# Low parts of 44 weight tiles made by ScalarE and an adding DMA instead of VectorE, with changed numbers and a changed choice in the instruction scheduler

## The chip, the cores and the metric

One core of one Trainium2 chip runs the whole program. The metric is the device time of one execution in microseconds. Five engines take part: PE (TensorE, matmuls), DVE (VectorE), ACT (ScalarE), POOL (GpSimd) and SP (SyncE, which begins the loads). Each engine works through its own list of instructions in order and waits at the head of the list for what other engines must deliver.

## What is computed

The reference is a chain of two blocks on 512 tokens of width 1024, in float32. The part that matters here is layer A of the second block:

```
u, qm, gate = split_cols(x @ a_w_in, (2 * 1536, 512, 2048))
a, gl = split(u, 2)                       # 1536 channels each
h = a * sigmoid(gl)
h = depthwise_conv(h, 31 taps, causal) + conv_b
y_mix = silu(layer_norm(h, g, b))         # over the 1536 channels
y_mem = memory cross attention of qm      # 4 heads
y = concat(y_mix, y_mem) * silu(gate)
x = layer_norm(ALPHA * x + y @ a_w_out)
```

Ahead of it stand a state-space mixer, a cross attention and a gated feed-forward layer; behind it stands layer B (an attention over selected keys).

## The kernel before

Activations lie with channels on the 128 partitions and the 512 tokens along the free dimension. A dense layer is done in tiles of 128 output channels: one tile of weights is 128 x 1024 numbers (512 KB), and `dense` runs 24 matmuls on it (8 slices of the input, 3 matmuls each: high part by high part, high by low, low by high), since float32 values are carried as two parts of a shorter type. `prep` makes the two parts: SP loads `raw`, ACT copies it to the high part `whi`, and DVE subtracts, `wlo = raw - whi`. There are 3 buffers for `raw` and 4 each for `whi` and `wlo`. PSUM has three banks `mm` for dense tiles, two each of `A` and `B`, one `C`.

Layer A takes 44 such tiles with the names `a_gl`, `a_a` (12 each), `a_qm` (4) and `a_gate` (16). `conv_tile` treats 128 channels: two dense tiles, then the 31 taps, of which ACT makes 11 products that POOL adds up (10 additions of 128 x 512), PE does one with a diagonal matrix into a bank `B`, and DVE does 19 in that bank. `LN` then centres the tiles and adds up their squares on POOL. When all 12 tiles are through, `lnc.finish` makes the statistics (matmuls into `C`), two rows are spread over the partitions, DVE and ACT normalise the 12 tiles, POOL multiplies by the gates, and the output layer `a_wo` follows.

The order of the instructions isn't that of the code. Every call is recorded as an `Op` with an estimated duration; `order` places them by a list schedule, engine by engine, with due times that are improved in `FBI` = 12 rounds by a schedule of the reversed program (`latest`); `emit` keeps the best round and issues the instructions in its order. All of them bear the line of `emit` in the profile (L378), so the rows are told apart by the names of their tiles. A number behind a name, as in `wlo1640`, is the number under which the tile was recorded; `raw1638`, `whi1639` and `wlo1640` are the three buffers of one tile of weights. Memory for a tile is taken when its first instruction is issued, and an instruction that finds no free buffer or bank waits.

Of the kernel before, what the change touches and what calls it, by code (L numbers as in the profile page):

```python
# [27 lines left out]
BIG = 1e30  # L28
WAHEAD = 400
WINDOW = 1500  # L30
SSD = 600
# [16 lines left out]

# [1 line left out]
ENGINES = ("PE", "ACT", "DVE", "POOL", "SP")  # L50
SWITCH, FBI, LATE, REUSE, MIX = 40000, 12, 850, 160, 0.5
LATENCY = {("PE", "PE"): 0.0, ("ACT", "ACT"): 0.0, ("DVE", "DVE"): 130.0, ("POOL", "POOL"): 102.0,
# [6 lines left out]
class View:  # L59
    """a lazily resolved access pattern of a tile"""  # L60

# [55 lines left out]
class Op:  # L117
    __slots__ = ("eng", "fn", "args", "kw", "outs", "ins", "deps", "succ", "prio", "dur", "port", "table", "new", "need", "idx",
                 "start", "end", "tiles", "m")


class Program:
    """records instructions in program order, then orders each engine's by a list schedule"""

# [12 lines left out]
    def rec(s, eng, fn, m, args, kw):  # L137
# [27 lines left out]
        if eng == "PE":  # L165
            one = m == "transpose" or args[1].base.dt == F32R
            o.table = n > 8
            o.dur = n / 2.4 * 2 if m == "transpose" else max(107, n / 2.4) + 2.5 if one else max(27, n / 2.4) * 4
        elif eng == "ACT":
            ptr = sum(isinstance(kw.get(k), View) for k in ("scale", "bias", "accum_out"))  # L170
            o.dur = n * 0.833 + 93 + 93 * ptr - 40 * (isinstance(args[1], View) and args[1].base.psum)
            o.table = _TABLE.get(args[2])
        elif eng == "DVE":
            two = m in ("tensor_tensor", "scalar_tensor_tensor")
            psum = any(x.psum for x in o.tiles)
            wide = [x for x in ins if int(np.prod(x.shape[1:])) > 1]
            ptr = len(ins) - len(wide)
            if m == "reciprocal":
                o.dur = n * 8.3 + 60
            elif m in ("tensor_reduce", "max", "match_replace"):  # L180
                o.dur = int(np.prod(wide[-1].shape[1:])) * 1.042 + 68
            elif not two and not psum:
                o.dur, o.port = n * 0.521 + 68 + 61 * ptr, n > 8
            else:
                o.dur = n * 1.042 + 68 + 61 * min(ptr, 1)
                o.port = two and sum(not x.base.psum for x in wide) == 2 and n > 8
        elif eng == "POOL":
            o.dur, o.port = (958 if kw.get("op") == ALU.pow else n * (2.2 if len(ins) > 1 else 1.0) + 99), n > 8
        else:
            o.dur = n * int(out.shape[0]) * 4 / 360.0  # L190
# [5 lines left out]
    def latest(s, prio):  # L196
        """latest starts, from a list schedule of the reversed program"""
        ops = s.ops
# [7 lines left out]
        while events:  # L206
# [4 lines left out]
            for e, q in ready.items():  # L211
                if busy[e] > now or not q:
                    continue
                o = ops[q[0][1]]
                if o.port and port > now:
                    heapq.heappush(events, port)
                    continue
                heapq.heappop(q)
                end = now + (o.dur + 1500 if e == "SP" else o.dur)
                busy[e] = now + o.dur  # L220
                if o.port:
                    port = end
                heapq.heappush(events, busy[e])
                when[o.idx] = -end
                for d in o.deps:
                    when[d] = max(when[d], end + s.latency(ops[d], o))
                    need[d] -= 1
                    if need[d] == 0:
                        heapq.heappush(wait, (when[d], -prio[d], d))
                        heapq.heappush(events, when[d])  # L230
        return when

    def order(s, prio, window):
# [4 lines left out]
        for o in ops:  # L238
            for x in o.tiles:
                left[x] = left.get(x, 0) + 1  # L240
                first.setdefault(x, o.idx)
                last[x] = o.idx
        # slots in use if the rest ran in program order: a tile may take one early only if this never exceeds the number there is
        live = {g: np.zeros(len(ops) + 1, np.int32) for g in free}
# [17 lines left out]
        while len(seq) < len(ops):  # L262
# [29 lines left out]
            for e, q in ready.items():  # L292
# [47 lines left out]
                if e == "SP":  # L340
                    hw = max(now, hw) + 450
                    dma = max(hw + 650, dma) + dur
                    o.end = dma + LATE
                    busy[e] = now + 60
                else:
                    o.end = now + dur
# [10 lines left out]
        return seq, max(o.end for o in ops), [o.start for o in ops]  # L357

    def emit(s, window):
        def real(a):  # L360
# [5 lines left out]
        prio = [o.prio * 200.0 for o in s.ops]  # L366
        best = r = s.order(prio, window)
        for it in range(FBI):
# [3 lines left out]
            r = s.order(w, window)  # L372
            if r[1] < best[1]:
                best, prio = r, w
        for o in best[0]:
# [5 lines left out]
def body(ctx, tc, t, out):  # L381
# [37 lines left out]

# [1 line left out]
    mhalf = const("mhalf", (P, 1))  # L421
# [21 lines left out]

# [1 line left out]
    def prep(src, kt, w=P):  # L445
        raw = new(wp, (P, 8 * P), F32, "raw")
# [5 lines left out]
        S.activation(hi[:, :n], raw[:, :n], AF.Copy)  # L452
        V.tensor_tensor(lo[:, :n], raw[:, :n], f(hi[:, :n]), op=ALU.subtract)
        prog.shift -= WAHEAD
# [13 lines left out]
    def wrange(name, mt, kt, k0=0):  # L468
        r = []
        while kt > 0:  # L470
            n = min(kt, 8)
            r += prep(t[name][mt][:, k0 * P:(k0 + n) * P], n)
            k0 += n
            kt -= n
        return r
# [17 lines left out]

# [1 line left out]
    def tok_sum(tiles, n=T):  # L495
# [27 lines left out]
    class LN:  # L523
        """layer norm over tiles that come one by one, centred first by the mean of the first npil tiles, whose sum is then 0"""

# [28 lines left out]
        def finish(s):  # L554
            """broadcast rows r, q with norm = centred * r - q"""
            ps = bank("C")
# [34 lines left out]
    NOFF, NPE = 11, 1  # L591
    # ================= block 1, mixer =================
    def load_x():
# [25 lines left out]

    # time steps of all heads  # L620
    raw = act()[:, :P]
# [28 lines left out]
    V.tensor_tensor(v3(dtr), v3(dtr), dtb.rearrange("p (o k) -> p o k", o=1).to_broadcast([P, 4, 16]), op=ALU.add)  # L650
    # softplus(x) = max(x, 0) + log1p(exp(-|x|)), log1p(e) = 2 atanh(e / (2 + e))
    ex, den, s2, po = s64(), s64(), s64(), s64()
# [18 lines left out]
    acs, cdec, dec = den, s2, s64()  # L671
    # cumulated steps as rows of heads
    ps = bank("B")[0:16, :]
# [14 lines left out]

    # causal convolution of xs, B, C; order of the channel tiles: B0 B1 C0 C1, then xs
    conv = {}  # L690
# [13 lines left out]

    # z gate
    zs = []
# [5 lines left out]

    # B in token rows, B C products
    triu_b = triu.rearrange("p (o k) -> p o k", o=1).to_broadcast([P, 4, P])
# [83 lines left out]

    # multi-scale pool
    icnt = const("icnt", (P, 64))  # L800
# [56 lines left out]

    # keys and values of the first memory
    def load_mem(src):
# [74 lines left out]

    # normalised SSD branch
    yhl = [split_g(conv[j], vc("ssd_norm", j)) for j in range(8)]
# [10 lines left out]

    # ================= block 1, cross attention =================
    def cols(x, b):
        return [a[:, b * P:(b + 1) * P] for a in x]  # L950

    class XAttn:
        """two heads (2 pr, 2 pr + 1) of 4; q: nd tiles [dims, T] per head; scale(tb): a number or a column per token"""

# [56 lines left out]
    def weave(*lists):  # L1011
        """emits the lists of steps in turns, each spread evenly over the longest"""
        n = max(len(x) for x in lists)
# [39 lines left out]

    # ================= block 1, swiglu =================
    rB = tok_bcast(rsq(tok_sum([ss.acc]), D, EPS))
# [23 lines left out]

    # taps of layer A: sigmoid(x) = (1 + tanh(x / 2)) / 2, and the half goes to the taps; some as diagonal matrices  # L1080
    cwh = vec2[:, 0:372]
# [38 lines left out]

    # ================= final norm of block 1 =================
    rB = tok_bcast(rsq(tok_sum([ss.acc]), D, EPS))
# [6 lines left out]
    MS = 128.0 ** -0.5  # L1129
    # ================= block 2, layer A =================  # L1130
    K0 = NOFF + NPE if NPE else NOFF + 1
# [39 lines left out]
    def gate_tile(w, j, half=False):  # L1171
        """silu(gate); with half, twice that from tanh"""
        ps = dense(wrange(w, j, 8), u)
# [13 lines left out]
    def out_tile(w, j, part, first, ln=None):  # L1187
        """part: the operands by row tile"""
        ks = sorted(part)
# [35 lines left out]

    # ================= block 2, layer B =================
    NQ0 = 6
# [101 lines left out]

    # token rows for the last layer norm  # L1330
    yN = [[act(), act()] for _ in range(4)]
# [48 lines left out]

    # last projection, token rows
    grow, brow = [act(), act()], [act(), act()]
# [151 lines left out]
```

## Time and profile before

| | before |
|---|---|
| timed runs | 1705.31, 1707.87, 1709.99 us (median 1707.87) |
| profiled execution, first to last instruction | 1705.8 us |
| median of the timed runs less that span | 2.1 us |
| PE busy | 1665.2 us (98%) |
| DVE busy | 1142.2 us (67%) |
| ACT busy | 775.9 us (45%) |
| POOL busy | 421.0 us (25%) |
| DMA engines busy, queue of the loads | 28.2% |

No time is given for the profiled execution beside its span, so sums are made in the span, and the 2.1 us to the median are added at the end. Busy shares are means over stages with different limits; an engine that is 67% busy overall can be full for a long stretch. PE's busy time is that of overlapping, pipelined matmuls, so a busy PE may still run at half its clock.

### The profile page before, as it was taken

The numbers are of one execution on the slowest core, as the hardware profiler recorded it, in microseconds if no ns is written. First come the engines' busy times: TensorE is split into PE (matmuls) and PEld (weight loads), VectorE is DVE, ScalarE is ACT, GpSimd is POOL, SyncE is SP. The second block draws the span as 40 slices with busy tenths as digits, with TensorE's granted clock in tenths as the row PEclk, the third lists the DMA queues.
The fourth block names the chain that finished last, engine by engine and source line by source line (L and its number), as shares of the span: only waits on it lengthen the run. The fifth ranks groups of instructions, "written<-read, shape, count | busy, mean of one in ns | idle before, by whom it ended". The sixth has DMA issues, their size and how long they took to land. (4 is left out here: it accounts for less than half of the span.)

```text
span 1705.8 us, 21241 instructions
## 1 busy us (share of the span) xinstructions
PE 1665.2 (98%) x7966; PEld 1361.4 (80%) x7966; DVE 1142.2 (67%) x1801; ACT 775.9 (45%) x1349; POOL 421.0 (25%) x325
## 2 busy tenths in 40 slices
PE   9999999999999999999999997999899999999998
PEld 7888678888888888888878775778787788788886
DVE  7836778574565435544477999988747895467754
ACT  6722444444553222332356766545435434545541
POOL 1004433020031001201233678965630000000000
PEclk9999999999999999999999998999999999999999
DMA  7321212531242333322323311232233123211121
GB/s 242 117 86 56 93 50 87 160 99 50 75 131 93 98 99 99 95 79 90 117 91 108 102 56 50 81 127 87 75 124 115 62 99 94 80 63 50 53 84 50
DMA packets 49719, 156.32 MB, mean 92 GB/s; under 512 B 5648, under 2 KB 7568, under 8 KB 49616
## 3 DMA queue, kind: packets, MB, share of 16 engines
q1 hardware_dynamic: 49616, 154.96, 28.2%
q8 instruction: 63, 1.03, 0.3%
q14 instruction: 40, 0.33, 0.1%
HBM read 152.71 MB, written 2.10 MB: 91 GB/s over the span
## 5 line engine op out<-in xcount | busy, mean ns | idle before, releaser
L378 PE MATMUL mm<-act,whi 128*128 128x512 f32 (+1 forms) x3888 | 1194.3, 388 | 18.5 <-DVE act L378 12.9
L378 PEld LDWEIGHTS mm<-act,whi 128*128 128x128 f32 x3888 | 717.8, 189 | 174.3 <-ACT act L378 15.3
L378 PE MATMUL mm<-act,wlo 128*128 128x512 f32 (+1 forms) x1944 | 749.4, 388 | 9.8 <-DVE wlo L378 9.6
L378 ACT ACTIVATE whi<-raw 128x1024 fp32r<-128x1024 f32 (+3 forms) x293 | 289.4, 991 | 582.0 <-PE mm L378 352.5
L378 POOL TENSOR_TENSOR act<-act,act 128x512 f32<-128x512 f32 (+1 forms) x252 | 372.5, 1493 | 683.7 <-DVE act L378 314.8
L378 DVE TENSOR_TENSOR wlo<-raw,whi 128x1024 fp32r<-128x1024 f32 (+3 forms) x293 | 373.2, 1281 | 123.7 <-ACT whi L378 118.9
L378 PEld LDWEIGHTS mm<-act,wlo 128*128 128x128 f32 x1944 | 366.9, 189 | 85.5 <-DVE wlo L378 11.3
L378 DVE TENSOR_TENSOR act<-mm,act 128x512 f32<-128x512 f32 (+3 forms) x173 | 114.6, 664 | 244.9 <-PE mm L378 236.9
L378 ACT ACTIVATE act<-act 128x512 f32<-128x512 f32 (+2 forms) x222 | 134.7, 617 | 104.6 <-DVE act L378 65.9
L378 DVE SCALAR_TENSOR_TENSOR B<-pad,vec,B 128x512 f32<-128x512 f32 x228 | 167.2, 753 | 5.7 <-PE B L378 1.5
L378 DVE TENSOR_TENSOR act<-act,act 128x512 f32<-128x512 f32 (+3 forms) x203 | 138.3, 711 | 26.2 <-ACT act L378 25.3
L378 POOL TENSOR_TENSOR fr<-fv,mhalf 128x1 f32<-128x1 f32 x4 | 2.2, 547 | 410.5 <-DVE fv L378 410.5
L378 ACT ACTIVATE act<-pad,vec 128x512 f32<-128x512 f32 x144 | 94.8, 730 | 11.6 <-DVE pad L378 11.4
L378 PE MATMUL A<-act,act 128*128 128x256 f32 (+6 forms) x488 | 97.8, 342 | 0.3
L378 PEld LDWEIGHTS A<-act,act 128*128 128x128 f32 (+1 forms) x488 | 72.1, 189 | 16.7 <-issue 5.6
L378 PE MATMUL mm<-whi,act 128*128 128x512 f32 x264 | 85.0, 393 | 0.0
L378 ACT ACTIVATE act<-C 128x128 f32<-128x128 f32 (+4 forms) x164 | 52.2, 359 | 70.6 <-PE C L378 68.3
L378 PE MATMUL B<-act,act 128*128 128x128 f32 (+2 forms) x492 | 71.0, 284 | 0.0
L378 PEld LDWEIGHTS B<-act,act 128*128 128x128 f32 (+1 forms) x492 | 61.7, 167 | 9.6 <-issue 3.4
L378 ACT ACTIVATE act<-mm 128x512 f32<-128x512 f32 (+3 forms) x92 | 51.7, 566 | 18.4 <-PE mm L378 18.3
L378 PEld LDWEIGHTS mm<-whi,act 128*128 128x128 f32 x264 | 49.4, 188 | 9.6
L378 PE MATMUL mm<-wlo,act 128*128 128x512 f32 x132 | 51.8, 393 | 0.0
(130 smaller groups left out, 965.6 us busy)
## 6 DMA issues: line engine op xcount, KB each, us to landing
raw<-in_w_g_dram SPq DMA_DIRECT2D x22, 512.0 KB, 3.3
raw<-in_w_u_dram SPq DMA_DIRECT2D x22, 512.0 KB, 3.3
raw<-in_w_om_dram SPq DMA_DIRECT2D x16, 512.0 KB, 3.8
raw<-in_w_d_dram SPq DMA_DIRECT2D x16, 512.0 KB, 3.5
raw<-in_a_gate_dram SPq DMA_DIRECT2D x16, 512.0 KB, 3.4
raw<-in_b_gate_dram SPq DMA_DIRECT2D x16, 512.0 KB, 3.3
raw<-in_b_wo_dram SPq DMA_DIRECT2D x16, 512.0 KB, 3.3
raw<-in_w_xbc_dram SPq DMA_DIRECT2D x12, 512.0 KB, 4.2
```

The source lines that it names most:

```text
L378: r = o.fn(*[real(a) for a in o.args], **{k: real(v) for k, v in o.kw.items()})
```

## The change

For the 44 tiles `a_gl`, `a_a`, `a_qm` and `a_gate`, DVE's subtraction goes. ACT writes the negated, rounded weights into `wlo` (a copy with scale -1), and a DMA begun by POOL reads the weights from DRAM a second time and adds them to `wlo` in place. All other tiles keep the subtraction. The scheduler gets other numbers (matmul durations, the time a load takes to land, POOL's rates, and a DMA begun by POOL held at 1100 ns on that engine), and of the 13 rounds it keeps the one for which a new function, `replay`, which runs each engine's list strictly in order, gives the shortest program.

```
+ADDED = ("a_gl", "a_a", "a_qm", "a_gate")
...
-SWITCH, FBI, LATE, REUSE, MIX = 40000, 12, 850, 160, 0.5
+SWITCH, FBI, LATE, REUSE, MIX = 40000, 12, 1500, 160, 0.5
...
-            o.dur = n / 2.4 * 2 if m == "transpose" else max(107, n / 2.4) + 2.5 if one else max(27, n / 2.4) * 4
+            o.dur = 109.0 if m == "transpose" else max(112.0, n / 2.4 + 16) if one else 2 * max(111.0, n / 1.2 + 2)
...
+        elif m == "dma_start" and eng == "POOL":
+            o.dur, o.bytes = 1100.0, n * int(out.shape[0]) * 8 / 360.0
         elif eng == "POOL":
-            o.dur, o.port = (958 if kw.get("op") == ALU.pow else n * (2.2 if len(ins) > 1 else 1.0) + 99), n > 8
+            o.dur, o.port = (1000 if kw.get("op") == ALU.pow else n * (2.35 if len(ins) > 1 else 1.0) + 99), n > 8
...
                     busy[e] = now + 60
+                elif o.m == "dma_start":
+                    busy[e] = now + o.dur
+                    dma = max(busy[e] + 650, dma) + o.bytes
+                    o.end = dma + LATE
...
+    def replay(s, seq):
+        free, end, left = dict.fromkeys(ENGINES, 0.0), {}, {}
...
+        for o in seq:
+            now = free[o.eng]
+            for d in o.deps:
+                now = max(now, end[d] + s.latency(s.ops[d], o))
+            for x in o.new:
+                taken[x.tag] += 1
+                if taken[x.tag] > s.bufs[x.tag]:
+                    now = max(now, heapq.heappop(back[x.tag]) + REUSE)
...
+        return max(end.values())
...
-        best = r = s.order(prio, window)
+        r = s.order(prio, window)
+        best, least = r, s.replay(r[0])
         for it in range(FBI):
...
             r = s.order(w, window)
-            if r[1] < best[1]:
-                best, prio = r, w
+            t = s.replay(r[0])
+            if t < least:
+                best, least = r, t
...
-    def prep(src, kt, w=P):
+    def prep(src, kt, w=P, add=False):
...
         S.activation(hi[:, :n], raw[:, :n], AF.Copy)
-        V.tensor_tensor(lo[:, :n], raw[:, :n], f(hi[:, :n]), op=ALU.subtract)
+        if add:
+            S.activation(lo[:, :n], raw[:, :n], AF.Copy, scale=-1.0)
+            G.dma_start(lo[:, :n], src, accum_op=ALU.add)
+        else:
+            V.tensor_tensor(lo[:, :n], raw[:, :n], f(hi[:, :n]), op=ALU.subtract)
...
-            r += prep(t[name][mt][:, k0 * P:(k0 + n) * P], n)
+            r += prep(t[name][mt][:, k0 * P:(k0 + n) * P], n, add=name in ADDED)
```

The whole order of the program changes with it. Three places are shown.

The first is the ninth `a_gl` tile (`raw1638`, `whi1639`, `wlo1640`). On DVE before, its low part stands behind the taps of two convolution tiles, which alternate over 18 instructions (banks `B1571` and `B1609`; the last three are shown):

```order
L378 SCALAR_TENSOR_TENSOR B1609_8371<-pad1597_7986,vec2_73,B1609_8371 128x512
L378 SCALAR_TENSOR_TENSOR B1571_8261<-pad1559_7775,vec2_73,B1571_8261 128x512
L378 SCALAR_TENSOR_TENSOR B1609_8371<-pad1597_7986,vec2_73,B1609_8371 128x512
L378 TENSOR_TENSOR wlo1640_8439<-raw1638_8153,whi1639_8233 128x1024
L378 TENSOR_TENSOR wlo1644_8441<-raw1642_8248,whi1643_8313 128x1024
L378 TENSOR_TENSOR wlo1582_8447<-raw1580_8110,whi1581_8341 128x512
```

With the change ACT writes both parts of that tile, behind the high parts of two attention outputs (`act1574`, `act1578`):

```order
L423 ACTIVATE act1574_8461<-act1573_8458 128x512
L423 ACTIVATE act1578_8469<-act1577_8466 128x512
L423 ACTIVATE wlo1640_8519<-raw1638_8490 128x1024
L423 ACTIVATE whi1639_8526<-raw1638_8490 128x1024
L423 ACTIVATE whi1643_8545<-raw1642_8495 128x1024
L423 ACTIVATE wlo1644_8555<-raw1642_8495 128x1024
```

And POOL's list, which before held only additions and short fills there, has the adding DMAs between the additions of the convolution (`act1598`) and the centring of finished tiles (those that read `act1611`, the mean):

```order
L423 TENSOR_TENSOR act1598_8369<-act1598_8369,act1608_8425 128x512
L423 MEMSET pad1764_8530 128x30
L423 DMA wlo1640_8519<-in_a_gl_dram 128x1024
L423 TENSOR_TENSOR act1375_7449<-act1375_7449,act1598_8369 128x512
L423 DMA wlo1644_8555<-in_a_a_dram 128x1024
L423 TENSOR_TENSOR act1323_7046<-act1323_7046,act1611_8581 128x512
L423 TENSOR_TENSOR act1363_7276<-act1363_7276,act1611_8581 128x512
```

What moved: the low part has left DVE's list, and is now made by two lists in turn, ACT's and POOL's.

The second place is on PE, the end of the memory attention of layer A. The rows into `C` turn the probabilities of one block of tokens, and ACT copies them out of the single bank `C` after each; `A1572` and `A1576` are two of its outputs. Before:

```order
L378 MATMUL C1549_8344<-ident_74,act1546_8041 128x128 x2
L378 MATMUL mm1425_8010<-act1312_6896,whi1423_7624 128x512
L378 MATMUL C1549_8344<-ident_74,act1546_8041 128x128 x2
L378 MATMUL mm1425_8010<-act1311_6890,wlo1424_7641 128x512
L378 MATMUL A1572_8359<-act1534_8012,act1290_7315 128x512
L378 MATMUL mm1645_8369<-act1297_6810,whi1643_8313 128x512
```

With the change:

```order
L423 MATMUL B1609_8372<-pad1597_7945,act860_4670 128x512
L423 MATMUL C1543_8399<-ident_74,act1510_8036 128x128 x4
L423 MATMUL C1548_8420<-ident_74,act1541_8125 128x128 x4
L423 MATMUL C1549_8435<-ident_74,act1546_8226 128x128 x4
L423 MATMUL A1572_8445<-act1534_8362,act1290_6987 128x512
L423 MATMUL A1572_8445<-act1535_8365,act1291_6991 128x512
L423 MATMUL A1576_8453<-act1536_8391,act1290_6987 128x512
```

What moved: three turns of `C` and the output behind them now follow each other with no dense matmul in between.

The third place is on PE too, the statistics of the convolution's layer norm (`C1826`), between matmuls of gate tiles (`mm1786`, `mm1791`, `mm1781`). Before:

```order
L378 MATMUL mm1786_9412<-act1311_6890,wlo1785_9447 128x512
L378 MATMUL mm1791_9515<-act1297_6810,whi1789_9397 128x512
L378 MATMUL C1826_9517<-ones_76,act1696_9194 128x1 x4
L378 MATMUL mm1791_9515<-act1298_6827,whi1789_9397 128x512
L378 MATMUL C1826_9517<-ones_76,act1614_8762 128x1 x4
```

With the change:

```order
L423 MATMUL mm1786_9492<-act1297_6894,whi1784_9410 128x512
L423 MATMUL mm1781_9488<-act1297_6894,wlo1780_9377 128x512
L423 MATMUL mm1781_9488<-act1299_6908,whi1779_9363 128x512
L423 MATMUL C1826_9499<-ones_76,act1696_9130 128x1 x4
L423 MATMUL mm1781_9488<-act1300_6919,whi1779_9363 128x512
```

What moved: the statistics come 43 rows of PE earlier. The first `a_gl` and `a_a` tiles end 51 rows later, since more of the layer ahead is done first. Between the end of the first `a_a` tile and the statistics PE has 1,013 dense matmuls of 512 columns where it had 1,105; from the statistics to the first matmul of `a_wo` it has 90 of them where it had 47 (and 65 of 256 columns where it had 80).

## Rows read from the trace of the kernel before

**Rows 1.** Page, part 1: busy time, share of the span, instructions.

```profile
PE 1665.2 (98%) x7966; PEld 1361.4 (80%) x7966; DVE 1142.2 (67%) x1801; ACT 775.9 (45%) x1349; POOL 421.0 (25%) x325
```

**Rows 2.** Busy time of each engine by stretch; columns in the first row.

```profile
core 0: us, PE busy (x) PEld busy (x) DVE busy (x) ACT busy (x) POOL busy (x), PEclk, DMA share, GB/s
500.00:850.00 350.00, 350.00 (x1553) 290.00 (x1552) 167.21 (x169) 113.00 (x150) 42.77 (x36) 1.00 0.30 95
850.00:880.00 30.00, 27.52 (x171) 23.94 (x171) 19.97 (x29) 13.46 (x22) 4.51 (x3) 1.00 0.37 123
880.00:1178.70 298.70, 283.93 (x1229) 224.31 (x1228) 273.93 (x358) 182.53 (x318) 214.35 (x159) 0.98 0.27 86
1178.70:1211.00 32.30, 26.36 (x165) 24.11 (x164) 26.96 (x40) 20.01 (x30) 22.67 (x6) 0.91 0.26 81
1040.00:1050.00 10.00, 2.32 (x6) 1.83 (x7) 10.00 (x15) 2.79 (x6) 9.92 (x7) 0.56 0.07 24
```

**Rows 3.** PE in order of time: start, us, instruction, [idle before, releaser].

```profile
880.02 0.39 PE L378 MATMUL mm<-whi,act 128*128 128x512 f32 x1
...
1047.68 0.79 PE L378 MATMUL mm<-act,wlo 128*128 128x512 f32 x1 [9.23 <-DVE wlo L378]
...
1051.77 0.63 PE L378 MATMUL mm<-act,whi 128*128 128x512 f32 x2
...
1178.69 0.50 PE L378 MATMUL C<-ones,act 128*128 128x1 f32 x4
...
1207.70 0.55 PE L378 MATMUL mm<-act,whi 128*128 128x256 f32 x1 [5.94 <-DVE act L378]
```

**Rows 4.** DVE in order of time, around the longest wait of PE.

```profile
1034.54 11.96 DVE L378 SCALAR_TENSOR_TENSOR B<-pad,vec,B 128x512 f32<-128x512 f32 x18
1046.41 2.96 DVE L378 TENSOR_TENSOR wlo<-raw,whi 128x1024 fp32r<-128x1024 f32 x3
```

**Rows 5.** Waits of SP's DMA queue, 880 to 1210 us: total, times, longest.

```profile
SPq L378 <- DVE wlo L378: 313.2, 55, 26.6
```

**Rows 6.** Chain that ended last, 1222 to 1252 us: start, us, what.

```profile
1225.94 24.77 PE mm L378 x108
```

**Rows 7.** Groups by shape, 880 to 1178.7 us: count, busy us, mean ns, idle before.

```profile
L378 DVE SCALAR_TENSOR_TENSOR B<-pad,vec,B 128x512 f32<-128x512 f32 x228 | 167.2, 753 | 5.7 <-PE B L378 1.5
L378 DVE TENSOR_TENSOR wlo<-raw,whi 128x1024 fp32r<-128x1024 f32 x44 | 62.5, 1440 | 3.1 <-ACT whi L378 2.9
L378 ACT ACTIVATE whi<-raw 128x1024 fp32r<-128x1024 f32 x45 | 47.4, 1059 | 70.6 <-PE mm L378 49.4 <-issue 7.0 <-DVE act L378 5.5
L378 POOL TENSOR_TENSOR act<-act,act 128x512 f32<-128x512 f32 x151 | 213.8, 1437 | 95.8 <-ACT act L378 86.4 <-DVE act L378 4.7
```

**Rows 8.** POOL in order of time: start, us, instruction, [idle before, releaser].

```profile
833.63 1.31 POOL L378 TENSOR_TENSOR act<-act,act 128x512 f32<-128x512 f32 x1 [2.77 <-ACT act L378]
...
882.45 2.67 POOL L378 TENSOR_TENSOR act<-act,act 128x512 f32<-128x512 f32 x2 [23.63 <-ACT act L378]
...
1173.84 1.29 POOL L378 TENSOR_TENSOR act<-act,act 128x512 f32<-128x512 f32 x1 [2.89 <-DVE act L378]
...
1189.35 15.12 POOL L378 TENSOR_TENSOR act<-act,act 128x512 f32<-128x512 f32 x1 [6.88 <-ACT act L378]
```

**Rows 9.** POOL's short instructions, groups by shape over the whole span.

```profile
L378 POOL TENSOR_TENSOR rn<-rv,mhalf 128x4 f32<-128x4 f32 x7 | 8.1, 1151 | 73.6 <-DVE rv L378 73.6
L378 POOL COPY act<-act 128x1 f32<-128x1 f32 x8 | 4.8, 595 | 87.1 <-DVE act L378 80.1 <-PE mm L378 4.7 <-ACT whi L378 2.2
```

**Rows 10.** DMA: KB each and median us to landing; queue's packets, MB, share.

```profile
raw<-in_a_gl_dram SPq DMA_DIRECT2D x12, 512.0 KB, 3.4
...
q1 hardware_dynamic: 49616, 154.96, 28.2%
```

**Rows 11.** PE in order of time: two turns of the bank C.

```profile
989.95 0.60 PE L378 MATMUL C<-ident,act 128*128 128x128 f32 x4
...
991.55 0.60 PE L378 MATMUL C<-ident,act 128*128 128x128 f32 x4
```

More of the change, by code (lines that the diff above doesn't have):

```diff
@@ L118 @@
     __slots__ = ("eng", "fn", "args", "kw", "outs", "ins", "deps", "succ", "prio", "dur", "port", "table", "new", "need", "idx",
-                 "start", "end", "tiles", "m")
+                 "start", "end", "tiles", "m", "bytes")
 class Program:
@@ L218, in latest @@
                 heapq.heappop(q)
-                end = now + (o.dur + 1500 if e == "SP" else o.dur)
+                end = now + (o.dur + 2150 if e == "SP" else o.dur + o.bytes + 2150 if o.m == "dma_start" else o.dur)
                 busy[e] = now + o.dur
@@ L357, in order @@
         return seq, max(o.end for o in ops), [o.start for o in ops]
+    def replay(s, seq):
+        free, end, left = dict.fromkeys(ENGINES, 0.0), {}, {}
+        back, taken, last = {g: [] for g in s.bufs}, dict.fromkeys(s.bufs, 0), {}
+        port, hw, dma = {"POOL": 0.0, "DVE": 0.0}, 0.0, 0.0
+        for o in seq:
+            for x in o.tiles:
+                left[x] = left.get(x, 0) + 1
+        for o in seq:
+            now = free[o.eng]
[5 more added lines that the diff above has]
+                    now = max(now, heapq.heappop(back[x.tag]) + REUSE)
+            if o.port:
+                now = max(now, port["DVE" if o.eng == "POOL" else "POOL"])
+            free[o.eng] = fin = now + o.dur
+            if o.eng == "SP":
+                hw = max(now, hw) + 470
+                dma = max(hw + 650, dma) + o.dur
+                fin, free["SP"] = dma + LATE, now + 470
+            elif o.m == "dma_start":
+                dma = max(fin + 650, dma) + o.bytes
+                fin = dma + LATE
+            if o.port:
+                port[o.eng] = fin
+            end[o.idx] = fin
+            for x in o.tiles:
+                left[x] -= 1
+                last[x] = max(last.get(x, 0.0), fin)
+                if left[x] == 0 and x.alloc is not None:
+                    heapq.heappush(back[x.tag], last[x])
+        return max(end.values())
     def emit(s, window):
```

## Prediction

> **What bounds the kernel now.** I read the page first: PE is busy 98% of the span [rows 1], so no more than some 40 us can be won without less work for PE, and the question is where those 40 us lie. The second view is the busy time by stretch [rows 2]. From 500 to 850 us PE never stops and DVE is half idle. Then comes layer A. PE is idle 30.00 - 27.52 = 2.48 us from 850 to 880, 298.70 - 283.93 = 14.77 us from 880 to 1178.7 and 32.30 - 26.36 = 5.94 us up to 1211: 23.2 of the 40 us lie here. DVE is busy 273.93 of the 298.7 us (92%), POOL 72%, ACT 61%: DVE is the crowded engine of this stage alone.
>
> The third view is PE in order of time, for what ended its waits [rows 3]. The longest, 9.23 us, ends with a `wlo` of DVE. DVE wasn't idle: it ran 18 taps for 11.96 us, and only then the subtraction [rows 4]. In the order these are the taps of `B1571` and `B1609`, and the part is `wlo1640`, so a low part that PE wanted stood in line behind convolution work. The second wait, 5.94 us at 1207.70, ends with DVE too. Behind this lies a slower effect: SP's loads waited 313.2 us in 55 waits for `wlo` subtractions, since `raw` is free only when DVE has read it [rows 5].
>
> The waits cost more than their length. In the ten microseconds of the long one the granted clock is 0.56 [rows 2], mostly the lower level of 1.2 GHz, and from 1047.68 to 1051.77 us PE needs 4.09 us for 9 matmuls [rows 3], 0.454 us each, where 108 in a row take 24.77 us, 0.229 each [rows 6]: 2.0 us lost. I take the same behind the second wait, whose stretch has a granted clock of 0.91 [rows 2]: 4 us for both.
>
> So the most that the change can return in this stage is 23.2 + 4.0 = 27.2 us, a span of 1678.6 us.
>
> **The change, part by part.** *DVE.* It loses 44 subtractions of 1.440 us [rows 7], 63 us; the row counts 44 of this size in the stretch of 298.7 us, but a few belong to other layers, and I take 40 of the change's: its load there falls from 273.9 to some 216 us, 76% of PE's 283.9. No low part of layer A stands behind taps any more.
>
> *ACT.* It gains 44 copies. The nearest row is its copy of the same tile, 1.059 us [rows 7]: 46.6 us, so 182.5 becomes some 226 us, 80% of PE's time. Covered as long as PE's matmuls take longer; the cover is thin, and ACT also empties banks for PE.
>
> *POOL.* It issues 44 DMAs, 37 of them between the first addition of the convolution and the last centring (counted in the order). No row shows such an issue. From below: a copy of one column takes 0.595 us, almost all of it fixed; from above: a power on 4 columns 1.151 us [rows 9], and an instruction that is locked out of memory by DVE takes longer still (first rival). I take 1.1 us, by the power, since writing out 128 rows of a transfer is more than a one-column copy. With 213.8 us for 151 additions [rows 7], less 10 us (an estimate: the mean of 1.437 stands beside 1.29 to 1.31 for a lone one [rows 8], 19 us over 151, and I give half of that to the subtractions that go), 1 us of fills and 37 x 1.1 = 41 us, POOL needs 246 us. It starts 2.4 us after the first `a_a` tile (882.45 against 880.02 [rows 3, 8]) and the statistics follow 3.6 us after its end (1178.69 against 1173.84 + 1.29): 252 us. PE's own work between those points was 283.9 us [rows 2] and has 92 matmuls of 0.229 us fewer, 21 us: 263 us. POOL is done 11 us ahead of PE, at 94% load. From the statistics to `a_wo` the chain took 1207.70 - 1178.69 = 29.0 us, 5.94 of them idle; in the new order PE has 43 more wide and 15 fewer narrow matmuls there, 43 x 0.229 less 15 of half that, 8 us, so 23.1 + 8 = 31 us of work cover it. The second wait goes.
>
> *The adding DMA.* A plain load of the tile lands 3.4 us after issue [rows 10]: the lower bound. It reads the weights and the old contents, so twice that, 6.8 us, is what I take. A `wlo` buffer is then held for the copy (1.06), POOL's turn (up to 1.44), the issue (1.1), the landing (6.8) and PE's 24 matmuls (5.5): 16 us. Four buffers against 5.5 us of PE for each tile allow 22 us, so the landing may grow to 12 us before PE waits for it each time.
>
> *Loads.* `raw` is freed by ACT's two copies instead of DVE's subtraction, so the waits for `wlo` [rows 5] shrink; no cost.
>
> *What stays or comes.* Three turns of the bank `C` now follow each other with nothing between. Two turns stood 1.60 us apart [rows 11], of which the four transposes take 0.60: 1.0 us of waiting, three times, 3 us. The ninth `a_gl` tile's low part follows `act1578` on ACT; from the end of `A1576` it needs DVE and ACT 1.7, the copy 1.06, the issue 1.1 and the landing 6.8, 11 us, against 10 us of matmuls in front of it: 1 us. Of the 2.48 us before 880, half, as the first inputs still come one by one from DVE. For the jitter of two engines at 80 and 94% I allow 4 us; from no row, but below it stands zero and above it the 14.8 us which DVE at 92% cost PE. Together 1.2 + 3 + 1 + 4 = 9.2 us.
>
> *Sum.* 27.2 - 9.2 = 18.0 us, a span of 1687.8 us, and with the 2.1 us from span to median **1690 us**. Outside layer A PE idles some 17 us with other causes; I move nothing there, though every list is reordered.
>
> **The rivals.** *POOL ends last (slower).* The 15.12 us that one addition took at 1189.35 [rows 8] show that POOL can be locked out while DVE runs operations with two inputs from memory back to back. If the issue of a DMA is held up like that, its price d rises, and everything behind it in POOL's list is late. The gain is gone when 2.4 + 203.8 + 1 + 37 d + 3.6 exceeds 263 by the 18 us that would be won: d = 1.9 us. At d = 2.3 the statistics come another 37 x 0.4 = 15 us later: 1723 us. For it: 94% load. Against it: the taps read one large operand from PSUM, and beside them the additions took 1.437 us, not 15.
>
> The Trainium skill, "SBUF — State Buffer", section "Who interferes with whom", speaks against the change: a DMA issued from GpSimd can't have its descriptors written while VectorE runs in a two-port mode, and the page's advice is to issue from another queue. By its list of operations (copies, casts, tensor_scalar) the taps would not do that, and by it the sum stays 1690 us; no run here shows an issue beside a tap, so the chance of this rival rests on the row above alone.
>
> *The DMA engines fill up (slower).* The queue spent 28.2% of 1705.8 us on 154.96 MB [rows 10], 1.63 us of all engines for one tile of 0.524 MB. At twice that the 44 additions take 143 us beside 0.27 x 298.7 = 81 us [rows 2]: 224 of some 284 us, and it fits. From (284 - 81) / 44 = 4.6 us each, 2.8 plain loads, it binds; at four plain loads (6.5 us) the stage takes 44 x 6.5 + 81 = 367 us instead of 298.7: 1776 us. Nothing in the profile prices an addition in flight.
>
> *The idle time moves to ACT or POOL (same).* ACT's list at 80% must feed POOL's additions, PE's banks and the new copies in turn. If that costs PE what DVE cost it, 14.8 us instead of 4, and the gaps bring the lower clock again (4 us), the gain is 18.0 - 10.8 - 4 = 3 us: 1705 us. For it: POOL waited 86.4 us for ACT [rows 7].
>
> *All goes as written (faster).* Only the three turns of `C` stay: 1678.6 + 2.1 + 3 = 1684 us.
>
> **How the numbers follow.** The forecast of 1690 us, with its neighbours from 1686 to 1697, has 0.48, and everything as written or still better, up to 1686, 0.14. A thinner gain, 1697 to 1702, has 0.14. No change, by idle time that moves or by d near 1.9, 0.11. POOL last 0.08, DMA engines full 0.05. A difference under 0.3% (5.1 us) can't be told from none here, so faster means below 1702.7: 0.48 + 0.14 + 0.14 = 0.76; same 0.11; slower 0.08 + 0.05 = 0.13. Below 1681 only the idle time of other stages is left to win (0.04), and of the slower cases I put 0.10 above 1709; the range from 1681 to 1709 leaves out these.
>
> **What would show it.** DVE's busy time from the first `a_gl` to the statistics near 216 us and no wait of PE on `wlo` of DVE there; ACT near 226 us; SP's waits for `wlo` a fraction of 313 us; the adding DMAs landing within 7 us; POOL's gaps at an issue near 1.1 us; PE's waits in layer A some 9 us in all, the clock at 1.00 in every stretch. The prediction is wrong if PE waits for `wlo` from a DMA tile after tile, if the statistics wait for POOL's centring, or if the gain lies in another stage.

## The result, and the profile after

The changed kernel takes **1734.61 us** (median of 4 runs, 1733.77 to 1734.88), the kernel before 1708.41 us (1705.31 to 1709.99) beside it: a ratio of 1.0155, 95% interval [1.014, 1.017]. It is 26 us slower, where 18 us less were forecast, and lies above the forecast range of 1681 to 1709 us. The profiled execution has a span of 1733.1 us, 27.3 us more than before.

The page of the changed kernel, parts 1 and 3 (beside [rows 1, 10]):

```profile
PE 1673.8 (97%) x7966; PEld 1367.2 (79%) x7966; DVE 1105.3 (64%) x1757; ACT 810.5 (47%) x1391; POOL 426.0 (25%) x369
...
q1 hardware_dynamic: 49616, 154.96, 27.7%
q0 software_dynamic: 6336, 23.07, 7.6%
```

The work moved as the diff says: DVE lost 37 us, ACT gained 35, POOL 5, and a second queue carries 23 MB. PE has the same 7966 matmuls but is busy 8.6 us longer and idle 59.3 us in place of 40.6.

To see where, I cut both spans at the same two points of the program: the first matmul of PE's diagonal taps (`B<-pad`) and the first column sum of the statistics. Busy time by stretch, first of before (bounds chosen anew, so these are not [rows 2]), then of the changed kernel; columns as in [rows 2]:

```profile
0.00:881.38 881.38, 873.16 (x4169) 716.83 (x4169) 516.71 (x706) 358.77 (x558) 152.83 (x137) 1.00 0.32 101
881.38:1178.69 297.31, 282.54 (x1222) 223.18 (x1221) 272.95 (x357) 181.14 (x317) 214.35 (x159) 0.98 0.27 87
1178.69:1705.80 527.11, 509.54 (x2578) 421.43 (x2576) 352.54 (x739) 235.95 (x476) 53.82 (x29) 0.99 0.24 78
```

```profile
0.00:893.18 893.18, 882.72 (x4216) 726.94 (x4217) 519.11 (x704) 364.76 (x567) 156.47 (x142) 0.99 0.33 104
893.18:1192.58 299.40, 270.58 (x1132) 210.40 (x1132) 227.35 (x312) 207.45 (x345) 227.70 (x198) 0.95 0.64 144
1192.58:1733.10 540.52, 520.55 (x2621) 429.83 (x2619) 358.88 (x741) 238.27 (x481) 41.87 (x30) 0.99 0.25 80
```

This is the whole result. The middle stretch has 90 matmuls fewer than before, 90 x 0.229 = 20.6 us of work moved to the two others, which duly grew by 11.8 and 13.4 us. But it did not get shorter: 299.4 us against 297.3, although DVE lost 45.6 us in it. What PE saved there became idle time (28.8 us in place of 14.8, so 14.0 more) and slow clock (270.58 us for what should be 282.54 - 20.6 = 261.9, so 8.6 more). With the 4.6 us (25.2 - 20.6) that the outer stretches lost, 27.3 us.

PE's longest waits of the changed kernel in order of time (beside [rows 3]):

```profile
1040.11 1.05 PE L423 MATMUL C<-ident,act 128*128 128x128 f32 x4 [3.12 <-ACT act L423]
...
1058.50 1.65 PE L423 MATMUL mm<-act,whi 128*128 128x512 f32 x3 [6.57 <-DVE act L423]
...
1097.28 0.80 PE L423 MATMUL mm<-act,wlo 128*128 128x512 f32 x1 [8.20 <-DVE wlo L423]
...
1230.47 0.79 PE L423 MATMUL mm<-act,whi 128*128 128x256 f32 x2 [5.35 <-ACT act L423]
```

None of them waits for an adding DMA. Two surprises stand in DVE's and POOL's lists. At 1087.94 one narrow subtraction of `a_wo`, which takes 0.68 us at its shortest in this stage, takes 9.28 us, while POOL runs seven additions in a row; PE stands 8.20 us for it. DVE, then POOL:

```profile
1087.94 9.28 DVE L423 TENSOR_TENSOR wlo<-raw,whi 128x512 fp32r<-128x512 f32 x1
```

```profile
1087.48 9.19 POOL L423 TENSOR_TENSOR act<-act,act 128x512 f32<-128x512 f32 x7
```

And from 1036 to 1060 us the three bank turns and the steps behind them stand alone on PE. Busy time of that stretch:

```profile
1036.00:1060.00 24.00, 11.64 (x26) 5.30 (x24) 21.43 (x30) 10.57 (x27) 19.58 (x17) 0.73 0.00 0
```

No byte moves in it (DMA share 0.00), PE is busy half the time, and its granted clock is 0.73 in the mean, between its two levels of 1.2 and 2.4 GHz.

### The profile page after: what moved, and what is told of

Read it like the earlier page. It is cut to its first block, busy times and chain, and to the rows that moved or that the text cites. A ratio compares the mean times of both kernels' runs of the same rounds, so it can differ in the third digit from the quotient of the medians.

```text
span 1733.1 us, 21288 instructions
## 1 busy us (share of the span) xinstructions
PE 1673.8 (97%) x7966; PEld 1367.2 (79%) x7966; DVE 1105.3 (64%) x1757; ACT 810.5 (47%) x1391; POOL 426.0 (25%) x369
## 5 line engine op out<-in xcount | busy, mean ns | idle before, releaser
L423 POOL TENSOR_TENSOR act<-act,act 128x512 f32<-128x512 f32 (+1 forms) x252 | 349.1, 1433 | 575.8 <-DVE act L423 330.5
L423 DVE TENSOR_TENSOR wlo<-raw,whi 128x1024 fp32r<-128x1024 f32 (+3 forms) x249 | 322.1, 1296 | 115.6 <-ACT whi L423 111.9
L423 ACT ACTIVATE act<-act 128x512 f32<-128x512 f32 (+3 forms) x222 | 133.8, 615 | 135.8 <-DVE act L423 100.1
L423 DVE TENSOR_TENSOR act<-act,act 128x512 f32<-128x512 f32 (+3 forms) x203 | 142.5, 731 | 32.0 <-ACT act L423 28.7
L423 PE MATMUL B<-act,act 128*128 128x128 f32 (+2 forms) x492 | 66.2, 286 | 0.6 <-DVE act L423 0.6
L423 PEld LDWEIGHTS B<-act,act 128*128 128x128 f32 (+1 forms) x492 | 57.8, 168 | 8.2 <-issue 2.8
L423 PE MATMUL C<-ident,act 128*128 128x128 f32 (+1 forms) x288 | 50.5, 283 | 8.7 <-ACT act L423 8.1
L423 ACT ACTIVATE act<-act,vec 128x512 fp32r<-128x512 f32 (+3 forms) x68 | 46.0, 699 | 20.4 <-DVE act L423 18.7
```

What stands on the lines that cost most here:

```text
L423: r = o.fn(*[real(a) for a in o.args], **{k: real(v) for k, v in o.kw.items()})
```

## The experiments

Three questions: does the adding or the new list cost the time; what is the adding worth if the list stays; are the named waits losses of their own. The kernel before took 1706.4 to 1708.1 us beside them.

**e1, e2: one half of the change each.** e1 is `ADDED = ()` in the changed kernel. e2 keeps the adding and takes back the scheduler:

```diff
-SWITCH, FBI, LATE, REUSE, MIX = 40000, 12, 1500, 160, 0.5
+SWITCH, FBI, LATE, REUSE, MIX = 40000, 12, 850, 160, 0.5
...
-            t = s.replay(r[0])
+            t = r[1]
```

(and the old durations of matmul, power, addition and landing).

> The changed kernel with no tile added by a DMA: the corrected scheduler and nothing else. Theory O (the new orders cost the time: three idle turns of the bank C, a subtraction shut out behind POOL's additions, waits in stages that hold no added tile): 1727 to 1742 us, about as slow as the change, with PE idle near 55 us. Theory D (the adding DMAs cost it: they land late, hold buffers and slow the plain loads): 1703 to 1713 us, as before, PE idle near 40 us.

> The scheduler of before, with its old constants and its own choice of the pass, and the 44 tiles added by DMAs. Theory O: the order is as good as that of before and DVE is relieved, 1685 to 1700 us. Theory D: 1725 to 1740 us, PE waits in layer A on low parts that come from a DMA. Theory S (every reordering scatters by tens of microseconds, whatever is changed): either, and the lost time lies in other stages than in the changed kernel.

e1: 1736.35 us, ratio 1.0167 [1.0149, 1.0186]. e2: 1724.60 us, 1.0096 [1.0080, 1.0111]. e1 comes out where O said, e2 0.4 us below the range of D, with three waits of PE of 1.7 to 3.5 us for an adding DMA; its longest wait, 9.90 us, ends with a subtraction shut out as in the change. Either half alone is slower, neither theory alone explains both, and the adding on top of e1 changes nothing that shows (1734.61).

**e3, e4, e9, e10, e16: other lists of the same kernel.** After a first list the scheduler makes twelve more in passes, and takes the one that it holds shortest. One line takes another (e4 as shown; in e9 and e10 `it == 9`, in e3 `it == 8`, in e16 `it == 10`):

```diff
-            if r[1] < best[1]:
+            if it == 7:
```

> The changed kernel, but with the list of another of the scheduler's passes (the ninth in place of the last), whose own estimate is 0.6 us longer (1694.24 against 1693.66). Theory S: the time differs from 1734.6 us by more than 8 us, most likely downwards. Theories O and D as steady effects: 1728 to 1741 us, with long waits in layer A again.

> The kernel before with the list of its eighth pass in place of the seventh, whose own estimate is 0.66 us longer (1601.72 against 1601.05). Theory S: it differs from 1708 us by more than 8 us. If the lists of one scheduler are alike in worth: 1703 to 1713 us.

> The kernel before with the list of its tenth pass, whose own estimate is 2.4 us longer than that of the list taken (1603.44 against 1601.05). Theory S (the lists scatter by tens of microseconds, and the list of before is a lucky one): 1715 to 1735 us. If the eighth pass was the exception: 1705 to 1714 us.

> e2 (scheduler of before, 44 tiles added by DMAs) with the list of its tenth pass, whose own estimate is 0.5 us longer. Theory S: 1710 to 1740 us, on either side of the 1724.6 us of e2, and in the mean of the lists the adding is worth nothing that shows beside the scatter. If the adding pays in the mean: below 1715 us.

> The changed kernel with the list of its eleventh pass, estimate 0.75 us longer (1694.41 against 1693.66). Theory S: 1715 to 1750 us, and the mean of the three lists with the adding lies within the scatter of those without. If the adding itself costs time in the mean: above 1745 us.

| scheduler | subtracted on DVE | added by DMA |
|---|---|---|
| of before | 1708.4 (before), 1728.65 (e4), 1723.90 (e9) | 1724.60 (e2), 1730.42 (e10) |
| corrected | 1736.35 (e1) | 1734.61 (the change), 1747.12 (e3), 1735.41 (e16) |
| corrected, short matmuls | 1733.30 (e18) | 1743.47 (e17) |

e4's ratio is 1.0117 [1.0100, 1.0134]: the unchanged kernel, with a list that the planner holds 0.66 us longer and in which some 6% of PE's instructions stand elsewhere (461 of 7966, by the names in the traces), is 20.7 us slower. The list of before is a favourable one: its two neighbours lie 16 and 21 us above it. It is also the one that its planner ranks first, but the first of the corrected planner (the change) is not measurably faster than a lower one (e16); three lists don't tell rank from chance. e9 is at 1.0099 [1.0077, 1.0122], e10 at 1.0134 [1.0114, 1.0155], e3 at 1.0225 [1.0210, 1.0241], upwards where I had thought downwards likelier. So the scatter of lists (21 us) is nearly as large as the whole loss (26 us), and theory S holds; e16, 1.0164 [1.0148, 1.0179], shows that two lists can also agree.

e15 was meant as a second list for e1, but the pass named is the one that e1 itself had taken: it is e1 again, 1738.05 us [1.0152, 1.0186], and tells only how well a time repeats.

> e1 (corrected scheduler, no adding DMA) with the list of the pass whose own estimate comes next, shorter by 0.5 us by one of its two estimates (1696.94 of the replay is the same as for e1's). Theory S: 1715 to 1750 us, anywhere by up to 15 us from the 1736.35 us of e1. If the corrected scheduler's lists are alike: 1731 to 1741 us.

**e5, e6, e7: the list held, the content exchanged.** PE's and SP's lists stay row by row. e5 and e6 write the low parts of the 44 tiles by copy and DMA in the list of before and of e4; e7 gives the subtractions back to DVE in the changed list, at the place of the copy. The lines that e5 adds where the lists are written out (`skip` holds the subtractions that go):

```diff
+            nc.scalar.activation(real(lo), real(raw), AF.Copy, scale=-1.0)
+            adds.append((max(t, now) + 1220, k, lo, src))
...
+            nc.gpsimd.dma_start(real(lo), real(src), accum_op=ALU.add)
...
+            if o.idx in s.skip:
```

> The order of before is kept row by row on PE and SP; only the 44 subtractions leave DVE's list, a copy on ACT stands right behind each high part, and the adding DMA on POOL 1.2 us later in the planner's time. Theory S (the adding is worth little or something, the loss of the change comes from its new lists): 1690 to 1710 us, and PE's wait at 1047.68 shrinks. Theory D (the adding itself costs): 1722 to 1745 us.

> The same on the list of e4, the eighth pass of before (1728.65 us without the adding). Theory S: 1710 to 1730 us. Theory D: 1740 us or more. Beside e5 this tells whether the worth of the adding hangs on the list.

> The order of the changed kernel is kept row by row on PE and SP; the 44 adding DMAs and negated copies go, and DVE subtracts at the place of the copy. Theory S: 1734 to 1750 us, since the list stays and DVE has its 63 us back. Theory D: 1708 to 1722 us.

e5: 1746.25 us, 1.0214 [1.0194, 1.0234]; e6: 1760.29 us, 1.0304 [1.0268, 1.0339]; e7: 1754.81 us, 1.0266 [1.0247, 1.0285]. In a list that wasn't planned for it the adding costs 38 and 32 us; in the one planned for it, taking it out costs 20. Two of the waits of PE in e5:

```profile
967.80 0.80 PE L410 MATMUL mm<-act,wlo 128*128 128x512 f32 x1 [3.48 <-DMA wlo<-in_a_gl_dram]
...
984.82 0.80 PE L410 MATMUL mm<-act,wlo 128*128 128x512 f32 x1 [2.77 <-DMA wlo<-in_a_gl_dram]
```

Nine such waits of 0.8 us or more sum to 21.0 us from 908 to 1156 us, of the 38. This is the price of latency: where DVE took 1.2 us, the low part now takes a copy, an issue and 7.8 us of landing, with four buffers as before. Theory S missed in all three. e6 lies in the range of theory D and e5 1.3 us above it, as if the adding itself cost the time; but e7, which takes it out, is slower still than the change, 4.8 us above the range of S and far from that of D. Read together, each content loses in the list that was planned for the other.

e7 also tells whose the second surprise is. The three bank turns and the step behind them keep PE idle for 3.12, 1.43, 0.88 and 6.57 us in the change, and for 2.83, 1.84, 0.88 and 6.57 us here, with no DMA added. The last of them:

```profile
1076.98 1.65 PE L429 MATMUL mm<-act,whi 128*128 128x512 f32 x3 [6.57 <-DVE act L429]
```

So these 12 us of idle time belong to the list and not to the adding. No run takes them out, and what they cost stays open.

**e8: 24 tiles more.** The changed list, and `a_wo` added too, at the place of DVE's subtraction:

```diff
-n, add=name in ADDED)
+n, add=name in ADDED, held=name == 'a_wo')
```

> The changed kernel with its order kept, but the 24 tiles of a_wo get their low parts by a copy on ACT and an adding DMA too, so that no subtraction of two operands from SBUF stands beside POOL's additions. Theory L (a lock-out of the subtraction behind POOL's additions costs the wait of 8.20 us): the wait at 1097.28 goes, 1722 to 1730 us. If the wait is the list's own, something else is late in its place: 1732 to 1740 us.

1771.95 us, 1.0371 [1.0351, 1.0391], far above both ranges. The shut-out subtraction is gone (a wide one is shut out for 8.74 us behind the statistics), and five waits for `a_wo`'s DMAs stand in its place before 1150 us, the longest:

```profile
1079.16 0.79 PE L451 MATMUL mm<-act,wlo 128*128 128x512 f32 x1 [8.08 <-DMA wlo<-in_a_wo_dram]
```

Latency again, so e8 couldn't judge theory L.

**e11, e14: the shut-out by itself.** e11 writes DVE's remaining subtractions in the form of the taps; e14 gives the eight narrow ones of `a_wo` to POOL, at their place in time; each replaces the operation where the lists are written out.

```diff
+            if o.m == "tensor_tensor" and o.args[0].base.tag == "wlo":
...
+                s.nc.vector.scalar_tensor_tensor(lo, raw, 1.0, hi, op0=ALU.mult, op1=ALU.subtract)
...
+                s.nc.gpsimd.tensor_tensor(lo, raw, hi, op=ALU.subtract)
```

> The changed kernel, order kept, with each subtraction that DVE still does for a low part written as a scalar_tensor_tensor (times 1.0, then subtract) in place of a tensor_tensor, the form of its taps. Theory L1 (only the tensor_tensor form is shut out behind POOL's additions): the 9.28 us of one subtraction goes and the wait at 1097.28 with it, 1720 to 1728 us. Theory L2 (any DVE operation with two operands in SBUF is shut out): one of 9 us again, 1731 to 1738 us.

> The changed kernel, order kept, but the eight narrow subtractions of a_wo in layer A (128x512) run on POOL in their place in time, 8 x 1.4 us more for POOL, so that none of them can be shut out behind POOL's additions. Theory L (the shut-out of 9.28 us is a loss of its own): the wait at 1097.28 shrinks to under 3 us, 1725 to 1730 us. Theory M: another wait takes its place, 1731 to 1740 us.

e11: 1734.32 us, 1.0156 [1.0139, 1.0174], and the same instruction takes 9.29 us:

```profile
1085.22 9.29 DVE L425 SCALAR_TENSOR_TENSOR wlo<-raw,whi 128x512 fp32r<-128x512 f32 x1
```

L1 falls: this other form is shut out too. e14: 1726.09 us, 1.0105 [1.0092, 1.0118], 8.5 us less than the change though POOL does more. On POOL the subtraction goes first and the seven additions follow:

```profile
1085.41 1.92 POOL L425 TENSOR_TENSOR wlo<-raw,whi 128x512 fp32r<-128x512 f32 x1
1086.67 9.37 POOL L427 TENSOR_TENSOR act<-act,act 128x512 f32<-128x512 f32 x7
```

The wait of 8.20 us is gone, and from 1069 to 1102 us PE has no other above 0.5 us in its place. Theory L holds: this wait was a loss of its own, a third of the 26 us. Seven more subtractions moved with it; the one by itself wasn't tried.

**e12, e13: the waits that the prediction counted, without any DMA.** In the kernel before, DVE's subtractions of the 44 tiles move forward to 1.2 us behind their high part (e12); or only that of the ninth `a_gl` tile, `wlo1640`, from behind the 18 taps of [rows 4] (e13). The two places of DVE's list in e13:

```diff
 TENSOR_TENSOR wlo1595<-raw1593,whi1594 128x1024
+TENSOR_TENSOR wlo1640<-raw1638,whi1639 128x1024
 SCALAR_TENSOR_TENSOR B1533<-pad1521,vec2,B1533 128x512
...
-TENSOR_TENSOR wlo1640<-raw1638,whi1639 128x1024
```

> The kernel before, order kept on PE, ACT, POOL and SP, no DMA added; only DVE's 44 subtractions of these tiles are moved forward in its list to 1.2 us after their high part in the planner's time. If the prediction read the wait at 1047.68 rightly (a low part in line behind 18 taps, 9.23 us and 2 us of slow clock): 1695 to 1702 us. If the time that DVE spends is what counts and not its place: 1703 to 1713 us.

> The kernel before with one instruction moved and nothing else: the subtraction of the ninth a_gl tile (wlo1640) goes from behind the 18 taps to 37 rows further forward in DVE's list, right behind its high part. Theory R (the prediction's reading of rows 3 and 4: the wait of 9.23 us is this place in line, and its 2.0 us of slow clock go with it): 1695 to 1699 us. Theory M (in a list this tight another wait takes its place, as in e12): 1703 to 1713 us.

e12: 1718.63 us, 1.0063 [1.0046, 1.0080], slower, and above both ranges. e13: **1707.58 us, 0.9994 [0.9986, 1.0003]**, nothing. Of the 9.23 us, PE's list in e13 shows this:

```profile
1025.75 1.10 PE L409 MATMUL B<-pad,act 128*128 128x512 f32 x2 [1.20 <-DVE pad L409]
...
1050.57 0.80 PE L409 MATMUL mm<-act,wlo 128*128 128x512 f32 x1 [4.23 <-DVE wlo L409]
...
1062.18 1.10 PE L409 MATMUL B<-pad,act 128*128 128x512 f32 x2 [2.97 <-DVE pad L409]
```

The next low part waits behind the same 18 taps, and two `pad` tiles that DVE writes are late now; the moved subtraction takes 2.29 us at its new place. Theory M holds: 4.23 + 2.97 + 1.20 = 8.4 us are back, and the stretch to the statistics takes 296.2 us in place of 297.3.

**e17, e18: one correction taken back.**

```diff
-            o.dur = 109.0 if m == "transpose" else max(112.0, n / 2.4 + 16) if one else 2 * max(111.0, n / 1.2 + 2)
+            o.dur = n / 2.4 * 2 if m == "transpose" else max(107, n / 2.4) + 2.5 if one else max(27, n / 2.4) * 4
```

> The changed kernel with one of the scheduler's corrections taken back: the planner again takes 0.216 us for a wide matmul in place of 0.229, so that it plans the other engines against a PE 6% faster than the chip's. All else as changed, the adding too. Theory P (the old lists are better because the plan asks more of DVE, ACT and POOL than PE needs, and the true durations leave no slack for what the plan leaves out): 1715 to 1730 us. If this correction is without effect: 1733 to 1748 us, among the lists of the corrected scheduler.

> e1 (no adding DMA) with the same correction taken back. Theory P: 1705 to 1728 us, among the lists of the scheduler of before. Otherwise 1733 to 1742 us, as e1 and e15.

1743.47 us, 1.0215 [1.0182, 1.0248], and 1733.30 us, 1.0151 [1.0132, 1.0171]. Neither lies in theory P's range, which speaks against the matmul's duration as what makes the corrected lists slower. One list of each doesn't exclude it: in e18 PE stands 15.62 us for a subtraction that is shut out for 6.83 us in place of 0.68, and had these 6 us come back as in e14, e18 would lie just inside P's range.

The stretch from the first `B<-pad` to the statistics, worked out as in the first section, for the runs that decide:

| kernel | stretch, us | matmuls of PE | PE idle | DVE busy | after it, us |
|---|---|---|---|---|---|
| before | 297.3 | 1222 | 14.8 | 273.0 | 527.1 |
| the change | 299.4 | 1132 | 28.8 | 227.4 | 540.5 |
| e1 | 306.1 | 1175 | 24.6 | 274.0 | 536.0 |
| e2 | 292.7 | 1118 | 27.1 | 228.0 | 539.9 |
| e4 | 303.8 | 1197 | 19.3 | 270.8 | 536.6 |
| e5 | 336.3 | 1222 | 37.8 | 225.3 | 527.5 |
| e7 | 307.9 | 1132 | 33.6 | 271.3 | 540.5 |
| e13 | 296.2 | 1223 | 13.2 | 273.7 | 529.5 |
| e14 | 286.7 | 1131 | 19.5 | 212.1 | 542.8 |

e4's loss isn't in one place: its stretch has 25 matmuls fewer and is still 6.5 us longer than that of before, and the parts ahead of it and behind it are 4.5 and 9.5 us longer.

## Why the prediction was wrong

**The step that failed** is the sum's first term: "So the most that the change can return in this stage is 23.2 + 4.0 = 27.2 us". It took PE's idle time in layer A for the price of DVE's load, so that a relieved DVE would give it back. e13 took the largest piece of it out of its line: by the prediction's reading 9.23 us and 2.0 us of slow clock should have come back, and 0.4 us did, within the interval of none. In the change DVE lost 45.6 us in the stretch, PE lost 20.6 us of work, and the stretch kept its length. DVE, ACT and POOL follow lists of their own, so an engine that is late at one row can hand its lateness to the next, and the row at which PE is seen to wait need not be the row that costs (e13), though it can be (e14).

**The second step** stands in one sentence of the prediction: "I move nothing there, though every list is reordered". The change's diff rewrites the list of every engine, and this alone can cost what the change cost. e4 moves some 6% of PE's instructions for 20.7 us; e1 rewrites the list without any adding for 28.4 us (1736.35 - 1707.93). I read the new list at three places and priced those. Its 90 moved matmuls I counted rightly (92), but used them only to compare PE with POOL and to cover the steps behind the statistics; the stretch that lost them didn't get shorter.

The terms one by one. DVE's load: 216 us forecast, 227.4 measured, though all 44 wide subtractions left the stretch where 40 were counted: the eight narrow ones take 16.3 us instead of 9.9, most of it the one shut out, and 16 other short operations 4.7 us more. ACT 226 forecast (46.6 on 182.5 would be 229), 207.5 measured, as only 38 of the copies fall into the stretch; POOL 246 against 227.7. None of the three fills its stretch (76, 69 and 76%), so their loads were less the wrong size than the wrong measure. Of the slow clock, the 9 matmuls counted behind the long wait are 10 in the trace, which makes the 2.0 us 1.8. The issue on POOL: 1.1 us taken, 0.88 measured in the median and 1.68 at most, so d never reached the 1.9 of the rival. Landing: 6.8 us taken; by the last part of the page:

```profile
raw<-in_a_gate_dram SPq DMA_DIRECT2D x16, 512.0 KB, 5.8
wlo<-in_a_gate_dram POOLq DMA_DIRECT2D x16, 512.0 KB, 7.8
```

7.4 in the median of all 44, 10.4 at most, under the 12 us at which PE would wait each time, and in the changed kernel no wait of PE ends with one; a single weight load waits 0.5 us. SP's waits for `wlo` on DVE fell from 313.2 [rows 5] to 116.4 us (893 to 1223 us), as said, but 103.8 for `whi` and 94.4 for the copies on ACT took their place. The second wait, 5.94 us, was to go; 2.30 and 5.35 us for ACT stand there now. The residue: three turns of `C` at 3.0 us were 3.12 + 1.43 + 0.88 = 5.4; for the jitter 4 us "from no row" were allowed. PE's idle time in the stretch, which was to fall, rose by 14.0 us, and 8.6 us of slow clock came with it. Of the 28.8 us that it is now, 12.0 stand at the turns of `C` and the step behind them and 8.2 at the shut-out; the sum had 3 us for all of this.

The rivals. POOL doesn't end last (its last addition ends 2.3 us ahead of the statistics, and PE comes to them without a wait), and the DMA engines don't fill: 7.6% of 1733.1 us for 44 tiles is 3.0 us each, near the 3.25 taken, and it binds only from 4.6. "The idle time moves to ACT or POOL" came nearest, with 3 us of gain where there were 26 of loss; it shared a chance of 0.11. None of the three signs came by which the prediction said that it would show itself wrong; what did show it were PE's waits in layer A and the clock, 28.8 us and 0.95 in the stretch where some 9 us and 1.00 were forecast. The rival that should have stood there is a plain one: a rewritten list lands anywhere in the scatter of lists, and that of before is the best of its kind that was measured.

What the parts cost, then. The kernel before lies 12 us under the mean of its scheduler's three lists (1720.3). The corrected scheduler's list lies 16 above that mean. The adding is worth nothing that shows: 1727.5 against 1720.3 in the mean with the old scheduler, 1739.0 against 1736.4 with the new, on lists that scatter by 6 to 21 us; shown is only that it pays in a list planned for it (e7) and costs in one that isn't (e5, e6). That e7's 20 us lie near the 18 forecast is chance: they are measured against a list that fits the adding, not against the kernel before. By e14 8.5 us of the loss are the shut-out. What makes the corrected scheduler's lists slower stays open: e17 and e18 speak against the matmul's duration, and of the other corrected figures and the new choice by replay none was tried alone. In the changed kernel the choice by replay plays no part: worked out from the kernel's code, its last pass is the shortest by the old measure too. A planner nearer the truth doesn't give the better list either: the corrected one plans 1693.66 us, the old one 1601.05. Nor is it settled which chain through the engines sets the 297 us of the stretch.

## What to carry to other kernels

When a change makes a planner write new lists, first time the old kernel with one or two neighbouring lists: their scatter (here 21 us) is the smallest effect that one list of each can show. Idle time before a row is a gain only if nothing else in that engine's list is late there too; move the one instruction by hand and time it before counting the sum. And a step taken off an engine at 92% is worth its place in the chain, not its length: what takes its place (here 1.2 us on DVE for some 10 us through ACT, POOL and a DMA) has to fit the buffers that were there.

## What the runs showed of the hardware

A subtraction with both operands in SBUF can be kept out for a whole run of POOL's additions, not only for one: 9.28 us behind seven of them in the change, 11.68 behind nine in e2, 10.23 behind eight in e10. e3, e8, e16 and e17 have such rows too, of 4.1 to 9.2 us, and e18, where no DMA is added, one of 6.83. Each of them ends 0.55 or 0.56 us (e8's wide one 1.09 us) after an addition behind which POOL begins no other at once. In the lists of the scheduler of before without the adding, in e1 and in e5 to e7 none took over 2.36 us, though POOL ran up to twenty additions in a row beside them (from 1078.86 us in the kernel before). The Trainium skill, "SBUF — State Buffer", section "Who interferes with whom", says that a VectorE instruction with two inputs in SBUF contends with a GpSimd instruction that reads SBUF; e11 agrees, with 9.29 us in another form of the subtraction. When it waits for one addition and when for a whole run of them no run tells.

An adding DMA of 512 KB takes 3.0 us of the 16 engines (7.6% of 1733.1 us for 44), a plain one 1.63 before, and slows its neighbours: the plain load of an `a_gate` tile lands in 5.8 us in the changed kernel, in 3.3 in e1, where nothing is added, and in 3.4 before:

```profile
raw<-in_a_gate_dram SPq DMA_DIRECT2D x16, 512.0 KB, 3.4
```
